# Up products of a hybrid trunk as pairs of 512 and 256 columns with a join, and later ticks for the residual's multiplications

## The chip, the cores and the metric

The kernel runs on one core of a Trainium2 chip. The metric is the device time of one execution in microseconds; before the change the median of three runs is 2261.07 us (2255.51 to 2263.56).

## What is computed

A trunk of two layers over 256 tokens of 2048 features, all in float32. Layer 0 mixes tokens with a bidirectional gated linear attention, layer 1 with a neighbourhood attention over a 4 x 64 grid; each mixer is followed by a gated ConvFFN, and each of the four sub-layers ends in x <- LayerNorm(alpha * x + f(x)). The part the change touches most is the ConvFFN:

```
def _conv_ffn(x, w_up, conv_w, conv_b, w_down):
    h = x @ w_up
    hp = jnp.pad(h, ((0, 0), (1, 1), (0, 0)))
    h = hp[:, :-2] * conv_w[0] + hp[:, 1:-1] * conv_w[1] + hp[:, 2:] * conv_w[2] + conv_b
    a, b = jnp.split(h, 2, axis=-1)
    return (jax.nn.gelu(a, approximate=False) * b) @ w_down
```

w_up has 2048 x 11264 entries, w_down 5632 x 2048.

## The kernel before

**Precision.** TensorE multiplies float32 operands that were rounded to a shorter form (`F32R`). So that little is lost, each operand is split in two: `hi`, its rounded value, made by an ACT copy (L182), and `lo`, what is left, made by a DVE subtraction (L183). A product is then three matmuls: hi by hi, hi by lo and lo by hi, summed in one PSUM bank.

**Weights.** The weights come as units of 128 x 2048 in the order of a plan (`unit_plan`). SP's queue loads them into three raw buffers; `emit_split` splits each into one of four pairs of `hi` and `lo` buffers. The split of a unit is issued when the unit four before it is done (`pump`, `finish`).

**Activations.** `xT` holds the transposed input of a sub-layer as [128, 16 slices of K, 2 token tiles, hi and lo, 128 tokens]; `gT` holds the second operand of the output and down products in the same form.

**Products with the weights held still.** Two helpers multiply a unit of 128 output columns (16 slices of K) by all 256 tokens. `ws_one` (with `ws_part`) serves the q and k units of both mixers: per slice of K one matmul of 512 columns, the `hi` weights by both halves of `xT` (hi and lo side by side), and one of 256, the `lo` weights by the hi half, into the hi half of the bank alone; the two halves of the bank are then added by a join (L578 on ACT, L579 on DVE). `ws_half` serves the up units: per slice three matmuls of 256 columns, all into the same 256 columns, so that nothing has to be joined.

**The ConvFFN.** A layer has 44 channels of 128 for each of the two halves a and b of h. The first two channels come from a block product with transposes (`pair`), the other 84 units from `up_one`, which calls `ws_half`. `evac` takes a unit out of PSUM: `conv` is one ACT pass (L754) and two DVE passes (L755, L756), then a GELU on ACT (L765) for a, and for b the product with the gate on DVE (L769) into `sums`. The down product of the first 32 channels is done in four portions of eight channels by a scheme of seven block products (`seven`, 12 matmuls of 512 columns each, L849) in place of eight; `operands` (L817 to L827) makes their operands from `sums` at the start of a portion. In a portion an up unit stands behind each `seven` unit; the first two up units come ahead of the first `seven`. The results are added to the residual `x_sb` by DVE (`into`, L835). After the portions there are eight more up units and an ordinary down product.

**LayerNorm between sub-layers.** `ln_mid` normalises `x_sb`, transposes it, and splits it into `xT`; the residual itself is multiplied by the norm's gain, four DVE multiplications for each of the two token tiles (`resid`, L392), and the norm's bias is added by a DMA of POOL's queue (L394). These steps are held back by a counter of ticks: `tick` counts pieces of matmul work, and at each tick at most one entry of `slow` that is due is issued.

**The attention.** For each of 16 heads POOL's queue loads a position bias (L896) and adds the mask to it by a second DMA (L897), into one buffer, so that a load waits for the scores of the head before. The scores (L919 and after, on DVE and ACT) need that bias, and TensorE's transposes of the probabilities (L937) need the scores.

**The order of the work.** The program hands its instructions to a scheduler, which sets the order on each engine by priority and by when it reckons that an operand is there; the place in the program is not always the place in an engine's order.

Of the kernel before, what the change touches and what calls it, by code (L numbers as in the profile page):

```python
# [10 lines left out]
F32 = mybir.dt.float32  # L11
# [3 lines left out]
ALU = mybir.AluOpType  # L15
AX = mybir.AxisListType

P = 128
D = 2048
T = 256  # L20
KC = D // P
# [86 lines left out]
def kernel(  # L108
# [16 lines left out]
    nc = tc.nc  # L125
# [15 lines left out]
    def ps_mm():  # L141
        return psum.tile([P, 512], F32, tag="mm", name="ps_mm", bufs=8 - TP)

    def ps_tp():
        return psum.tile([P, 512], F32, tag="tp", name="ps_tp", bufs=TP)

    raws, splits = {}, {}
    st = {"load": 0, "split": 0, "done": 0, "next": 0, "tick": 0}
# [32 lines left out]
    def emit_split(src, hi, lo):  # L181
        nc.scalar.copy(hi, src)  # L182
        nc.vector.tensor_tensor(lo, src, hi.bitcast(F32), ALU.subtract)  # L183
# [32 lines left out]
    def take():  # L216

        pump()
        j = st["next"]
        st["next"] = j + 1  # L220
        return splits.pop(j)

    def finish():
        st["done"] += 1
        pump()

    side, slow = [], []
# [8 lines left out]
    def tick():  # L236
        st["tick"] += 1
        while side and side[0][0] <= st["tick"]:
            side.pop(0)[1]()

        if slow and slow[0][0] <= st["tick"]:
            slow.pop(0)[1]()
# [5 lines left out]
    def mm(o, l, r, start, stop):  # L248
        nc.tensor.matmul(o, l, r, start=start, stop=stop)  # L249


    def ws_part(xs, hi, lo, ps, kcs):
        hi3 = hi.rearrange("p (k m) -> p k m", m=P)
        lo3 = lo.rearrange("p (k m) -> p k m", m=P)
        ps4 = ps.rearrange("p (t h n) -> p t h n", t=2, h=2)
        for kc in kcs:
            mm(ps, hi3[:, kc], xs[:, kc].rearrange("p t h n -> p (t h n)"), kc == 0, False)
            mm(ps4[:, :, 0], lo3[:, kc], xs[:, kc, :, 0], False, kc == KC - 1)

    def ws_half(xs, evac):  # L260

        hi, lo = take()
        ps = ps_mm()[:, :T]
        hi3 = hi.rearrange("p (k m) -> p k m", m=P)
        lo3 = lo.rearrange("p (k m) -> p k m", m=P)
        for kc in range(KC):
            mm(ps, hi3[:, kc], xs[:, kc, :, 0], kc == 0, False)
            mm(ps, hi3[:, kc], xs[:, kc, :, 1], False, False)
            mm(ps, lo3[:, kc], xs[:, kc, :, 0], False, kc == KC - 1)
            if kc % 4 == 3:  # L270
                tick()
        evac(ps)
        finish()

    def ws_one(xs, evac):
        hi, lo = take()
        ps = ps_mm()
        for c in range(4):
            ws_part(xs, hi, lo, ps, range(4 * c, 4 * c + 4))
            tick()  # L280
        evac(ps)
        finish()
# [58 lines left out]
    xT = act.tile([P, KC, 2, 2, P], F32R, tag="xT", name="xT")  # L341
# [12 lines left out]
    def ln_head(pool, xs, t, stats):  # L354
        mv = pool.tile([P, 2], F32, tag="ln_mv", name="ln_mv", bufs=2)
        nc.vector.bn_aggr(mv, stats)
        rstd = pool.tile([P, 1], F32, tag="ln_rs", name="ln_rs", bufs=2)
        rsqrt(rstd, mv[:, 1:2], 1.0, LN_EPS, pool)
        return mv, rstd

    def ln_mid(pool, xs, t, stats, idx, gb):

        def head():
            mv, rstd = ln_head(pool, xs, t, stats)
            for b in range(4):
                blk = xs[:, t, b * 512:b * 512 + 512]
                nc.vector.tensor_scalar(blk, blk, mv[:, 0:1], rstd, ALU.subtract, ALU.mult)  # L367

        cell = {}

        def turn(b):
            tp = ps_tp()
            for i in range(4):
                kc = 4 * b + i
                nc.tensor.transpose(tp[:, i * P:i * P + P], xs[:, t, kc * P:kc * P + P], ident)  # L375
            if b == 0:
                cell["f"] = pool.tile([P, 4, 4, P], F32, tag="x", name="ln_f")
            f = cell["f"][:, b]
            ks = slice(4 * b, 4 * b + 4)
            with tc.high_priority(offset=LN_BEFORE):  # L380
                for i in range(4):
                    kc = 4 * b + i
                    g_, b_ = lng_sb[:, idx, 0, kc:kc + 1], lng_sb[:, idx, 1, kc:kc + 1]
                    if i % 2 == 0:
                        nc.scalar.activation(f[:, i], tp[:, i * P:i * P + P], AF.Identity, bias=b_, scale=g_)
                    else:
                        nc.vector.tensor_scalar(f[:, i], tp[:, i * P:i * P + P], g_, b_, ALU.mult, ALU.add)  # L387
                emit_split(f, xT[:, ks, t, 0], xT[:, ks, t, 1])

        def resid(b):  # L390
            sl = slice(b * 512, b * 512 + 512)
            nc.vector.tensor_tensor(xs[:, t, sl], xs[:, t, sl], gb[:, sl], ALU.mult)  # L392
            if b == 3:
                nc.gpsimd.dma_start(xs[:, t], lnp[idx, 1:2, :].broadcast_to([P, D]), accum_op=ALU.add)  # L394

        later(head, 0)
        for b, n in enumerate((4, 0, 0, 0)):
            later(lambda b=b: turn(b), n)
        for b in range(4):
            slow.append((st["tick"] + 24 + 5 * b, lambda b=b: resid(b)))  # L400

    gb_ps = {}

# [124 lines left out]
    hi = hi_p.tile([P, 2048], F32R, tag="hi", name="hi")  # L528
    lo = lo_p.tile([P, 2048], F32R, tag="lo", name="lo")
# [211 lines left out]
    def ffn(layer):  # L741
        pool = scope["pool"]
        idx = 2 * layer + 1
# [5 lines left out]
        sums = pool.tile([P, PN, 2, P], F32, name="sums")  # L749

        def conv(i, ch, hh):
            c = pool.tile([P, T], F32, tag=f"c{i}", name="c", bufs=2)
            w_ = cw[:, ch]
            nc.scalar.activation(c, hh, AF.Identity, bias=cb[:, ch:ch + 1], scale=w_[:, 1:2])  # L754
            nc.vector.scalar_tensor_tensor(c[:, 1:], hh[:, :T - 1], w_[:, 0:1], c[:, 1:], ALU.mult, ALU.add)  # L755
            nc.vector.scalar_tensor_tensor(c[:, :T - 1], hh[:, 1:], w_[:, 2:3], c[:, :T - 1], ALU.mult, ALU.add)  # L756
            return c

        gate = {}

        def evac(i, ch, ps):

            c = conv(i, i * NCT + ch, ps)
            if i == 0:
                nc.scalar.activation(c, c, AF.Gelu)  # L765
                gate["a"] = c
            else:
                gg = sums[:, ch % PN]
                nc.vector.tensor_tensor(gg.rearrange("p t n -> p (t n)"), gate["a"], c, ALU.mult)  # L769
                if ch >= PN * (PORTIONS + 1):  # L770
                    k = ch - PN * PORTIONS
                    emit_split(gg, gT[:, k, :, 0], gT[:, k, :, 1])

        def up_one(i, ch):
            ws_half(xT, lambda ps: evac(i, ch, ps))


        ht = {}
# [100 lines left out]
        for ch in range(PN * (PORTIONS + 1), NCT):  # L879
            for i in range(2):  # L880
                up_one(i, ch)
# [187 lines left out]
```

## Time and profile before

| | |
|---|---|
| runs | 2255.51, 2261.07, 2263.56 us |
| profiled execution | 2262.09 us, span 2260.4 us |
| mean granted TensorE clock | 0.998 |
| TensorE busy | 2240.8 us (99%), 14236 matmuls |
| DVE busy | 1600.3 us (71%) |
| ACT busy | 1195.6 us (53%) |
| POOL busy | 151.8 us (7%) |
| DMA | 489.69 MB, 217 GB/s in the mean |

All times in the profile are counted from the start of the span. In a row of the timeline the first number is the start, the second the busy time of what the row holds (x2 is two instructions in a row), and brackets at the end say how long the engine was idle before and what ended it. Matmuls overlap in the pipeline, so that the spacing of their starts says what one costs, and the mean duration does not.

### The profile page before, as it was taken

The page shows a single profiled execution, that of the slowest core. Times are in us where ns is not written, and L with a number is a line of the kernel's source. Part 1 is how long each engine was busy: PE and PEld are TensorE (multiplying, and loading weights), DVE is VectorE, ACT ScalarE, POOL GpSimd, SP SyncE. Part 2 cuts the span into 40 slices and gives each one's busy share as a digit, 9 for nine tenths or more (in the row PEclk, how much of TensorE's full clock was granted, in tenths as well). Part 3 has the DMA queues.
Part 4 walks back from the last instruction along what each step waited for, and adds up shares of the span by engine and source line. Part 5 has one row for each costly group of instructions (what it writes and reads, how often), then busy time and mean ns, then how long its engine had stood idle before and what let it go on. Part 6 is the DMA issues. An engine that isn't in the chain of part 4 may idle for free. (4 is left out here: it accounts for less than half of the span.)

```text
span 2260.4 us, 34682 instructions
## 1 busy us (share of the span) xinstructions
PE 2240.8 (99%) x14236; PEld 2034.1 (90%) x14236; DVE 1600.3 (71%) x2144; ACT 1195.6 (53%) x1625; POOL 151.8 (7%) x200
## 2 busy tenths in 40 slices
PE   9999999999999999999999999999999999999998
PEld 7888888999999999999888888889999999999996
DVE  7656655877777777775676666667877778787765
ACT  6655543555555555554454554445655555555542
POOL 1101000000000000000010100000000000000001
PEclk9999999999999999999999999999999999999999
DMA  8544464858888787865475555547688787878742
GB/s 282 184 174 168 178 236 167 279 180 258 254 237 246 228 256 220 252 218 187 168 259 174 194 189 200 182 167 261 203 251 249 243 246 226 251 225 258 233 187 94
DMA packets 73535, 489.69 MB, mean 217 GB/s; under 512 B 8416, under 2 KB 10720, under 8 KB 15904
## 3 DMA queue, kind: packets, MB, share of 16 engines
q1 hardware_dynamic: 53424, 364.67, 43.6%
q0 software_dynamic: 19664, 122.28, 23.6%
q8 instruction: 112, 1.84, 0.3%
q10 hardware_dynamic: 288, 0.52, 0.1%
q14 instruction: 47, 0.39, 0.0%
HBM read 482.20 MB, written 2.10 MB: 214 GB/s over the span
## 5 line engine op out<-in xcount | busy, mean ns | idle before, releaser
L249 PE MATMUL ps_mm<-xT,hi 128*128 128x256 f32 (+1 forms) x6160 | 1252.8, 298 | 1.2 <-ACT hi L182 0.6
L183 DVE TENSOR_TENSOR lo<-raw,hi 128x1024 fp32r<-128x1024 f32 (+1 forms) x695 | 828.9, 1208 | 498.6 <-ACT hi L182 497.5
L182 ACT CAST hi<-raw 128x1024 fp32r<-128x1024 f32 (+1 forms) x695 | 708.3, 1038 | 757.9 <-PE ps_mm L249 550.6
L249 PEld LDWEIGHTS ps_mm<-xT,hi 128*128 128x128 f32 x6160 | 993.3, 191 | 45.4 <-ACT hi L182 1.8
L249 PE MATMUL ps_mm<-xT,lo 128*128 128x256 f32 x3472 | 981.0, 283 | 0.5 <-DVE lo L183 0.5
L249 PEld LDWEIGHTS ps_mm<-xT,lo 128*128 128x128 f32 x3472 | 663.9, 191 | 1.5 <-DVE lo L183 1.1
L849 PE MATMUL ps_mm<-hi,gT 128*128 128x512 f32 x896 | 295.6, 391 | 0.0
L249 PE MATMUL ps_mm<-hi,xT 128*128 128x512 f32 x896 | 283.8, 391 | 0.3 <-DVE xT L183 0.3
L249 PE MATMUL ps_mm<-hi,gT 128*128 128x512 f32 x896 | 278.3, 390 | 0.0
L249 PEld LDWEIGHTS ps_mm<-hi,xT 128*128 128x128 f32 x896 | 168.1, 188 | 35.6 <-DVE xT L183 1.1
L249 PEld LDWEIGHTS ps_mm<-hi,gT 128*128 128x128 f32 x896 | 168.2, 188 | 34.7
L849 PEld LDWEIGHTS ps_mm<-hi,gT 128*128 128x128 f32 x896 | 168.7, 188 | 33.0
L849 PE MATMUL ps_mm<-lo,gT 128*128 128x512 f32 x448 | 175.7, 392 | 0.0
L249 PE MATMUL ps_mm<-lo,xT 128*128 128x512 f32 x448 | 174.8, 390 | 0.0
L249 PE MATMUL ps_mm<-lo,gT 128*128 128x512 f32 x448 | 174.6, 390 | 0.0
L183 DVE TENSOR_TENSOR lo<-x,hi 128x1024 fp32r<-128x1024 f32 x128 | 151.5, 1218 | 5.6 <-ACT hi L182 5.1
L182 ACT CAST hi<-x 128x1024 fp32r<-128x1024 f32 x128 | 128.6, 1045 | 37.6 <-PE ps_mm L849 12.4
L249 PEld LDWEIGHTS ps_mm<-lo,gT 128*128 128x128 f32 x448 | 84.1, 188 | 17.0
L249 PEld LDWEIGHTS ps_mm<-lo,xT 128*128 128x128 f32 x448 | 84.2, 188 | 16.6
L849 PEld LDWEIGHTS ps_mm<-lo,gT 128*128 128x128 f32 x448 | 84.6, 189 | 13.3
L754 ACT ACTIVATE c<-ps_mm,cb,cw 128x256 f32<-128x256 f32 x168 | 94.1, 560 | 0.0
L835 DVE SCALAR_TENSOR_TENSOR x_sb<-x_sb,ps_mm 128x512 f32<-128x512 f32 x128 | 85.9, 676 | 0.0
(157 smaller groups left out, 1298.5 us busy)
## 6 DMA issues: line engine op xcount, KB each, us to landing
raw<-in_w_dram SPq DMA_DIRECT2D x340, 1024.0 KB, 4.9
x<-in_w_dram POOLq DMA_DIRECT2D x64, 1024.0 KB, 8.1
z<-in_w_dram POOLq DMA_DIRECT2D x32, 1024.0 KB, 8.1
x_sb<-in_lnp_dram POOLq DMA_DIRECT2D x6, 1024.0 KB, 11.1
g<-in_lnp_dram POOLq DMA_DIRECT2D x4, 1024.0 KB, 19.1
raw<-in_w_dram SPq DMA_DIRECT2D x12, 256.0 KB, 6.6
bt<-in_bias_dram POOLq DMA_DIRECT2D x16, 192.0 KB, 2.8
bt<-bmask_sb POOLq DMA_DIRECT2D x16, 192.0 KB, 3.3
```

Of the source, the lines that this page charges most:

```text
L182: nc.scalar.copy(hi, src)
L183: nc.vector.tensor_tensor(lo, src, hi.bitcast(F32), ALU.subtract)
L249: nc.tensor.matmul(o, l, r, start=start, stop=stop)
L754: nc.scalar.activation(c, hh, AF.Identity, bias=cb[:, ch:ch + 1], scale=w_[:, 1:2])
L835: nc.vector.scalar_tensor_tensor(blk, blk, ALPHA if first else 1.0, ps, ALU.mult, ALU.subtract if sub else ALU.add)
L849: nc.tensor.matmul(ps, o[:, kc, l], r[:, kc], start=new and kc == 0 and n == 0, stop=kc == 3 and n == 2, skip_group_check=not new)
```

## The change

Up units go through `ws_one` in place of `ws_half`, which falls away: 16 matmuls of 512 columns and 16 of 256 in place of 48 of 256. `evac` gets an argument `parts`: an ACT copy takes the second half of the bank to a new SBUF tile `h`, a DVE addition adds the first half to it in place, and the convolution reads `h` instead of the bank. The channels of `pair` still go to the convolution straight from their bank. The tile of the second gate half (`c1`) has one buffer in place of two. In `ln_mid`, for the norm between the first ConvFFN and the attention (`idx == 1`), the ticks at which the residual's multiplications come due are 36 + 8b in place of 24 + 5b.

```diff
@@ -256,21 +256,6 @@
         for kc in kcs:
             mm(ps, hi3[:, kc], xs[:, kc].rearrange("p t h n -> p (t h n)"), kc == 0, False)
             mm(ps4[:, :, 0], lo3[:, kc], xs[:, kc, :, 0], False, kc == KC - 1)
-
-    def ws_half(xs, evac):
-
-        hi, lo = take()
-        ps = ps_mm()[:, :T]
-        hi3 = hi.rearrange("p (k m) -> p k m", m=P)
-        lo3 = lo.rearrange("p (k m) -> p k m", m=P)
-        for kc in range(KC):
-            mm(ps, hi3[:, kc], xs[:, kc, :, 0], kc == 0, False)
-            mm(ps, hi3[:, kc], xs[:, kc, :, 1], False, False)
-            mm(ps, lo3[:, kc], xs[:, kc, :, 0], False, kc == KC - 1)
-            if kc % 4 == 3:
-                tick()
-        evac(ps)
-        finish()
...
@@ -397,7 +382,7 @@
         for b in range(4):
-            slow.append((st["tick"] + 24 + 5 * b, lambda b=b: resid(b)))
+            slow.append((st["tick"] + (36 + 8 * b if idx == 1 else 24 + 5 * b), lambda b=b: resid(b)))
...
@@ -749,7 +734,7 @@
         def conv(i, ch, hh):
-            c = pool.tile([P, T], F32, tag=f"c{i}", name="c", bufs=2)
+            c = pool.tile([P, T], F32, tag=f"c{i}", name="c", bufs=2 - i)
...
@@ -758,8 +743,15 @@
-        def evac(i, ch, ps):
-
+        def evac(i, ch, ps, parts=False):
+
+            if parts:
+                h = pool.tile([P, T], F32, tag="h", name="h", bufs=2)
+                h3 = h.rearrange("p (t n) -> p t n", t=2)
+                ps4 = ps.rearrange("p (t h n) -> p t h n", t=2, h=2)
+                nc.scalar.copy(h3, ps4[:, :, 1])
+                nc.vector.tensor_tensor(h3, ps4[:, :, 0], h3, ALU.add)
+                ps = h
             c = conv(i, i * NCT + ch, ps)
...
@@ -772,7 +764,7 @@
         def up_one(i, ch):
-            ws_half(xT, lambda ps: evac(i, ch, ps))
+            ws_one(xT, lambda ps: evac(i, ch, ps, True))
```

The order that the scheduler builds shows the change at three places. The lines of the changed kernel are lower by 15 from `ws_one` on, and by 8 after `evac`.

TensorE at the seam between a `seven` unit (L849, after the change L841) and the next up unit (L249), in the first portion; before:

```order
L849 MATMUL ps_mm<-lo,gT 128x512
L849 MATMUL ps_mm<-hi,gT 128x512
L249 MATMUL ps_mm<-xT,hi 128x256 x2
L249 MATMUL ps_mm<-xT,lo 128x256
L249 MATMUL ps_mm<-xT,hi 128x256 x2
L249 MATMUL ps_mm<-xT,lo 128x256
```

and after the change, in the same place:

```order
L841 MATMUL ps_mm<-lo,gT 128x512
L841 MATMUL ps_mm<-hi,gT 128x512
L249 MATMUL ps_mm<-xT,hi 128x512
L249 MATMUL ps_mm<-xT,lo 128x2x128
L249 MATMUL ps_mm<-xT,hi 128x512
L249 MATMUL ps_mm<-xT,lo 128x2x128
```

Each pair of 256-column products with the `hi` weights has become one of 512; nothing else on TensorE has moved between the units.

DVE at the start of the first ConvFFN's last portion, where `operands` (L819 to L827, after the change L811 to L819) follows the last up unit of the portion before; before:

```order
L183 TENSOR_TENSOR lo<-raw,hi 128x1024
L755 SCALAR_TENSOR_TENSOR c<-ps_mm,cw,c 128x255
L183 TENSOR_TENSOR lo<-raw,hi 128x1024
L756 SCALAR_TENSOR_TENSOR c<-ps_mm,cw,c 128x255
L769 TENSOR_TENSOR sums<-c 128x256
L819 TENSOR_TENSOR sums<-sums 128x4x128
L823 TENSOR_TENSOR sums<-sums 128x4x128
```

and after the change:

```order
L183 TENSOR_TENSOR lo<-raw,hi 128x1024
L753 TENSOR_TENSOR h<-ps_mm,h 128x256
L183 TENSOR_TENSOR lo<-raw,hi 128x1024
L740 SCALAR_TENSOR_TENSOR c<-h,cw,c 128x255
L741 SCALAR_TENSOR_TENSOR c<-h,cw,c 128x255
L761 TENSOR_TENSOR sums<-c 128x256
L811 TENSOR_TENSOR sums<-sums 128x4x128
L815 TENSOR_TENSOR sums<-sums 128x4x128
```

The addition of the join stands where the first pass of the convolution stood, between the two halves of a split, and both passes come behind the second half. On ACT the copy of the join stands between the two roundings of that split, and the convolution's pass behind the second.

DVE at the start of the attention, with the last of the residual's multiplications (L392, after the change L377) ahead of the first head's scores (L919, after the change L911); before:

```order
L392 TENSOR_TENSOR x_sb<-x_sb,g 128x512 x2
L183 TENSOR_TENSOR lo<-raw,hi 128x1024
L579 TENSOR_TENSOR qk<-ps_mm,join_t 128x256
L183 TENSOR_TENSOR lo<-raw,hi 128x1024
L183 TENSOR_TENSOR q<-qk,q 128x256
```

and after the change:

```order
L377 TENSOR_TENSOR x_sb<-x_sb,g 128x512 x2
L183 TENSOR_TENSOR lo<-raw,hi 128x1024
L564 TENSOR_TENSOR qk<-ps_mm,join_t 128x256
L183 TENSOR_TENSOR lo<-raw,hi 128x1024
L183 TENSOR_TENSOR q<-qk,q 128x256
```

From the end of the first ConvFFN to the end of the attention the rows of all five engines read alike, but for line numbers.

## Rows read from the trace of the kernel before

**Rows 1.** The page: busy time, share and count; the chain that ended last.
```profile
PE 2240.8 (99%) x14236; PEld 2034.1 (90%) x14236; DVE 1600.3 (71%) x2144; ACT 1195.6 (53%) x1625; POOL 151.8 (7%) x200
...
PE ps_mm L249 38%; PE ps_mm L849 7%; PE ps_tp L249 1%; DMA bt<-bmask_sb 0%; PE ps_tp L937 0%; PE ps_tp L375 0%; DVE lo L183 0%; DVE x_sb L367 0%; DVE ln_st L463 0%; DVE x_sb L417 0%; POOLq L1065 0%; DVE ln_f L387 0%; POOL x_sb L424 0%; PE ps_tp L790 0%; ACT x_sb L422 0%
```

**Rows 2.** Waits (total, times, longest): TensorE's longest in all; DMA's in 424 to 1066.
```profile
PE ps_tp L937 <- DVE s L930: 4.0, 1, 4.0
...
ACT hi L182 <- DMA raw<-in_w_dram: 9.2, 3, 4.7
...
ACT hi L182 <- DMA x<-in_w_dram: 2.7, 2, 2.0
```

**Rows 3.** Busy time by stretch: a portion, and four microseconds of the attention.
```profile
core 0: us, PE busy (x) PEld busy (x) DVE busy (x) ACT busy (x) POOL busy (x), PEclk, DMA share, GB/s
625.70:756.20 130.50, 130.50 (x939) 123.63 (x938) 101.29 (x128) 73.42 (x92) 9.16 (x12) 1.00 0.82 242
1190.70:1194.70 4.00, 4.00 (x17) 3.41 (x18) 2.47 (x5) 2.25 (x5) 0.86 (x1) 0.62 0.66 145
```

**Rows 4.** Timeline of TensorE: a `seven` unit, an up unit, the next `seven`.
```profile
902.39 0.62 PE L849 MATMUL ps_mm<-hi,gT 128*128 128x512 f32 x2
...
904.44 0.39 PE L849 MATMUL ps_mm<-hi,gT 128*128 128x512 f32 x1
904.67 0.40 PE L249 MATMUL ps_mm<-xT,hi 128*128 128x256 f32 x2
...
910.42 0.40 PE L849 MATMUL ps_mm<-hi,gT 128*128 128x512 f32 x1
```

**Rows 5.** Timeline of TensorE: 44 pairs of `ws_one` in the attention, behind 512-column matmuls.
```profile
1380.20 0.39 PE L249 MATMUL ps_mm<-xT,hi 128*128 128x512 f32 x1
...
1380.89 0.40 PE L249 MATMUL ps_mm<-xT,hi 128*128 128x512 f32 x1
...
1381.25 0.40 PE L249 MATMUL ps_mm<-xT,hi 128*128 128x512 f32 x1
...
1385.84 0.40 PE L249 MATMUL ps_mm<-xT,hi 128*128 128x512 f32 x1
...
1395.73 0.44 PE L249 MATMUL ps_tp<-k,q 128*128 128x256 f32 x2
```

**Rows 6.** Timeline of TensorE: eight pairs of `ws_one` behind 256-column products.
```profile
1270.46 0.39 PE L249 MATMUL ps_mm<-xT,hi 128*128 128x512 f32 x1
...
1273.23 0.87 PE L249 MATMUL ps_tp<-k,q 128*128 128x256 f32 x6
```

**Rows 7.** Groups of instructions: busy us, mean ns of one, idle before.
```profile
L754 ACT ACTIVATE c<-ps_mm,cb,cw 128x256 f32<-128x256 f32 x168 | 94.1, 560 | 0.0
...
L765 ACT ACTIVATE c<-c 128x256 f32<-128x256 f32 x88 | 36.4, 413 | 36.0 <-DVE c L756 36.0
...
L578 ACT COPY join_t<-ps_mm 128x256 f32<-128x256 f32 x48 | 17.4, 362 | 2.9 <-issue 2.1 <-PE ps_mm L249 0.8
...
L579 DVE TENSOR_TENSOR qk<-ps_mm,join_t 128x256 f32<-128x256 f32 x32 | 13.4, 420 | 0.1
```

**Rows 8.** Timeline of DVE inside a portion, after an up unit.
```profile
911.58 1.23 DVE L183 TENSOR_TENSOR lo<-raw,hi 128x1024 fp32r<-128x1024 f32 x1 [2.49 <-ACT hi L182]
912.73 0.47 DVE L755 SCALAR_TENSOR_TENSOR c<-ps_mm,cw,c 128x255 f32<-128x255 f32 x1
```

**Rows 9.** Timeline at a portion's start: DVE's last operand, TensorE's first `seven`.
```profile
890.92 0.68 DVE L183 TENSOR_TENSOR gT<-sums,gT 128x512 fp32r<-128x512 f32 x1
...
893.42 0.40 PE L849 MATMUL ps_mm<-hi,gT 128*128 128x512 f32 x1
```

**Rows 10.** Timeline of DVE and TensorE in the attention: the second head's scores.
```profile
1186.89 0.76 DVE L919 SCALAR_TENSOR_TENSOR s<-ps_tp,bt 128x256 f32<-128x256 f32 x2 [7.17 <-DMA bt<-bmask_sb]
...
1191.51 0.52 PE L249 MATMUL ps_mm<-xT,hi 128*128 128x512 f32 x1
...
1194.59 0.60 PE L249 MATMUL ps_mm<-xT,hi 128*128 128x512 f32 x1
```

## The prediction

> **What bounds the kernel now.** Read the page's busy shares first: TensorE is busy for 2240.8 of 2260.4 us, DVE for 71% of the span, and the chain that ended last consists of TensorE's matmuls at L249 and L849 [rows 1]. A busy TensorE is not yet a TensorE that works at the shortest spacing, so the second view is what it waits for: in the whole program one wait of 4.0 us, in the attention, and in the first ConvFFN's 642 us ACT waited 9.2 + 2.7 us in all for weights that a DMA brought, TensorE not at all [rows 2]. The third is a table by stretch: one ConvFFN portion is 130.50 us long, TensorE fills it, and DVE has 101.29 us of work in it, ACT 73.42, the DMA engines a share of 0.82 [rows 3]. So in the ConvFFN the time is the number of matmuls times their spacing, and the spacing is read from starts in the timeline, not from the mean durations of the groups (those overlap).
>
> There a `seven` unit's nine 512-column matmuls from 902.39 to 904.44 take 2.05 us, 0.228 each; the up unit behind it starts at 904.67 and the next `seven` unit at 910.42: 5.75 us for 48 matmuls of 256 columns, 0.120 each [rows 4]. Half the columns cost more than half the time: 2 x 0.120 = 0.240 against 0.228.
>
> **The change, part by part.**
>
> *The matmuls.* An up unit issues, for each of 16 slices of K, two products of 256 columns with the same weights and one with others. Now the two are one of 512 columns: 48 matmuls become 32, the columns stay. The attention's q and k units already run that form, through `ws_one`, so its price is in the trace. Where such a run follows 512-column matmuls, as nearly all up units do (behind `seven`, or behind another up unit), the first pair starts at 1380.20 and the seventeenth at 1385.84: 5.64 us for the 16 pairs of a unit; 44 pairs to 1395.73 take 15.53 us, 0.353 each, so it does not drift [rows 5]. Behind the attention's short products of 256 columns, eight pairs from 1270.46 to 1273.23 take 2.77 us, 0.346 each [rows 6]. That makes 5.54 us a unit. I take 5.64, because what stands ahead of the up units is what stands ahead of the run in [rows 5]; 5.54 is the low bound. The high bound is the slowest pair in the timeline of that run: 1380.89 to 1381.25, 0.36, that is the 3 x 0.120 of now and no gain.
>
> The gain is 5.75 - 5.64 = 0.11 us for each of the 168 units (the count of L754 on `ps_mm` [rows 7]): **18.5 us**. By the two bounds: 168 x 0.21 = 35 us, and nothing.
>
> The Trainium skill speaks against this size. Its page "TensorE: Matmul & The Clock Gate", section "Back-to-back issue gap", gives N / 2.4 + 2.5 ns for a warm matmul: 109 ns for 256 columns and 216 for 512, so that the merger would save 2.5 ns a pair, 168 x 16 x 2.5 ns = 6.7 us (an estimate from that page). The trace shows 120 and 228 instead; the sum goes by the trace.
>
> *The join.* Each unit gets an ACT copy of 128x256 out of PSUM and a DVE addition. The same two stand in the attention at 362 and 420 ns [rows 7]. Per portion (16 units) that is 5.8 us of ACT and 6.7 of DVE: DVE goes to 108.0 of about 128.7 us, 84%, ACT to 79.2, 62% [rows 3, 7]. Within one pair of units DVE sits idle for 2.49 us until ACT's next rounding, whose own release is TensorE giving back a weight buffer [rows 8]; 0.42 more and 0.11 less length leave about 1.9. The splits of a unit start when the unit four before it is done, so they are ready units ahead. I cost the join at nothing; the cover is that idle time, and if it were gone each unit would pay up to 0.78 us, 168 x 0.78 = 131 us. It isn't gone unless DVE loses four times what the join adds.
>
> *The convolution* now reads SBUF where it read PSUM. L754 took 560 ns on PSUM; another ACT pass over 128x256 on SBUF, L765, took 413 [rows 7]. DVE's two passes on SBUF stand nowhere in the trace; between 0.42 (the addition) and their 0.47 now [rows 8]. All of it lies beside TensorE: nothing. The PSUM bank comes free after the addition instead of after the second pass, earlier. The second gate tile lost its spare buffer: its writer waits for the product of the channel before, which is a whole pair of units old.
>
> *The portion boundary* is where the longer way out of PSUM could reach TensorE. `operands()` needs the last channel's product, and the first `seven` unit needs the operands. The last of these ends at 890.92 + 0.68 = 891.60; TensorE takes up that unit at 893.42 [rows 9]. The slack is 1.8 us. The two up units in between shrink by 0.22, the join adds 0.36 + 0.42 = 0.78 (the order now has copy, rounding, convolution on ACT, and addition, split, the two passes on DVE, so part of it hides behind the split). 0.8 us remain: no wait.
>
> *The residual's multiplications.* The ticks of the eight DVE multiplications at the attention's start go from 24 + 5b to 36 + 8b. But the order built for DVE shows them at the very places they had before, ahead of the first head's scores, and from there to the attention's end no row of any engine or queue moved, POOL's and SP's DMAs included. The scheduler had pulled them forward and still does. I cost it at zero, and with it stays what goes wrong there: the bias of the second head lands late, DVE waits 7.17 us for it, TensorE 4.00 [rows 10], and then runs for some microseconds at a mean granted clock of 0.62 [rows 3], partly at the lower level, 1.2 GHz.
>
> **The sum** against the profiled execution, 2262.09 us (span 2260.4 and 1.7 around it): 2262.1 - 18.5 + 0 = 2243.6. That run lies 1.0 above the median of 2261.07, so the median should come to **about 2243 us**, -0.8%.
>
> **The rivals.**
>
> *The fast spacing everywhere.* If the up units settle at 0.346, as in [rows 6], the gain is 35 us: 2226. For it: the runs of the first FFN units follow short transposes. Against: nothing in [rows 5] leaves 0.353 in 44 pairs, and 140 of the 168 units come after the first `seven` of their layer, behind 512 columns or behind other up units.
>
> *Columns alone count.* If each pair took the 0.36 of the slowest pairs, or a matmul cost its columns and next to nothing beside, as the page named above has it, the time would be 2254 to 2261: no change. Against it stand 0.228 and 0.120 [rows 4], and that two of three pairs in [rows 5] are at 0.35.
>
> *Slower: the wait at the portion boundary.* If on ACT the copy falls behind one more rounding (1.05) and on DVE the addition behind one more split (1.22), the chain grows by 0.78 + 2.27 = 3.05, the slack of 1.6 is spent and TensorE waits 1.45 us at each of 8 boundaries. That alone is 12 us and would only halve the gain. It decides from 2.3 us a boundary (18.5 / 8), a chain longer by 3.9. With a wait like the attention's 4.0, and the slow pairs behind it (five take 3.08 us from 1191.51 to 1194.59 [rows 10], 1.3 more than at 0.353), a boundary costs 5.3 and all eight 42: about 2286. Against it: the order puts the addition directly behind the first split.
>
> *The change of ticks does act*, though no row moved: without the wait of 4.0 and the slow pairs the time would be 5.3 us lower still, 2238.
>
> **How the numbers follow.** Forecast 0.80; fast spacing everywhere 0.08; ticks that act 0.02; columns alone 0.05; part of the gain lost in boundary waits, so that less than 0.3% is left, 0.02; slower 0.03. A measurement of this kernel can tell about 0.3% (6.8 us) from no change. So faster 0.90, same 0.07, slower 0.03. The range: upward 4 us for half a microsecond at each boundary, and 4 for the spread of the runs (2255.51 to 2263.56): 2251. Downward 8 us if half of the units run at 0.346 (84 x 0.10), and 4 of spread: 2231.
>
> **What would show it.** TensorE should have 2688 matmuls fewer, and an up unit from its first matmul to the next `seven` should last 5.64 us (5.54 in the fast case, 5.75 if only columns count). A portion should last 128.7 us instead of 130.5. The matmuls at L849's place should start with no wait in the releasers, and DVE should still show idle time ahead of the first split of each pair. The wait of the second head should be there again, about 4 us. The prediction is wrong if a portion is longer than 130 us, if TensorE shows waits on DVE's operand splits, or if the sum of pairs is right and the attention or the seams between stages changed by several microseconds.

## Result and the profile after

The changed kernel takes **2246.93 us** in the median of five runs (2245.65 to 2247.35). The kernel before, run beside it, takes 2261.07 (2255.51 to 2263.56). The ratio is 0.9941, interval 0.9924 to 0.9958: faster by 14.1 us, 0.6%. The profiled execution took 2247.35 us (span 2245.6), 14.7 less than that of before.

Busy time in the changed kernel, from its profile page:

```profile
PE 2222.8 (99%) x11548; PEld 1889.9 (84%) x11548; DVE 1660.4 (74%) x2312; ACT 1258.2 (56%) x1793; POOL 150.8 (7%) x200
```

Against [rows 1], TensorE has 2688 matmuls fewer, which is 168 units of 16. DVE has 60 us more work and ACT 63, and TensorE is still the engine that is never free.

The timeline of TensorE, to be read beside [rows 4]: the last matmuls of a `seven` unit, the up unit, the next `seven` unit (L841 is L849 of before):

```profile
500.20 0.40 PE L841 MATMUL ps_mm<-hi,gT 128*128 128x512 f32 x1
...
502.93 0.39 PE L249 MATMUL ps_mm<-xT,hi 128*128 128x512 f32 x1
...
503.27 0.40 PE L249 MATMUL ps_mm<-xT,hi 128*128 128x512 f32 x1
...
503.62 0.40 PE L249 MATMUL ps_mm<-xT,hi 128*128 128x512 f32 x1
...
503.99 0.40 PE L249 MATMUL ps_mm<-xT,hi 128*128 128x512 f32 x1
...
508.57 0.40 PE L841 MATMUL ps_mm<-hi,gT 128*128 128x512 f32 x1
```

From 502.93 to 508.57 an up unit lasts 5.64 us (5.75 before). After the first of 0.34 the pairs in it take 0.35, 0.35 and 0.36 us by turns (starts are rounded to 0.01), 0.3525 in the mean; the run of [rows 5] has the same rhythm.

The groups of ACT and DVE that form and read the join, to be read beside [rows 7]:

```profile
L739 ACT ACTIVATE c<-h,cb,cw 128x256 f32<-128x256 f32 x168 | 101.1, 602 | 59.8 <-DVE h L753 59.6
...
L752 ACT COPY h<-ps_mm 128x256 f32<-128x256 f32 x168 | 61.4, 365 | 0.0
...
L741 DVE SCALAR_TENSOR_TENSOR c<-h,cw,c 128x255 f32<-128x255 f32 x168 | 80.4, 479 | 1.5
...
L753 DVE TENSOR_TENSOR h<-ps_mm,h 128x256 f32<-128x256 f32 x168 | 70.0, 417 | 0.0
```

Where the time went shows in a table by stretch, from the last transposes of a ConvFFN's first channels to its last down product (the first row is the first ConvFFN, the second row the second), and for the first four heads of the attention, from the first head's scores to the fourth's last product (third row). The first number after the window is its length. Before the change:

```profile
423.67:1126.13 702.46, 701.97 (x4989) 662.80 (x4988) 521.04 (x669) 380.79 (x485) 37.55 (x50) 1.00 0.75 232
1549.58:2249.49 699.91, 699.91 (x4973) 661.23 (x4972) 515.15 (x661) 376.13 (x478) 40.36 (x53) 1.00 0.74 228
1166.75:1221.94 55.19, 51.19 (x288) 44.32 (x286) 33.83 (x59) 28.19 (x52) 5.71 (x8) 0.97 0.68 224
```

and after it:

```profile
423.45:1116.57 693.12, 692.62 (x3654) 591.16 (x3652) 551.33 (x753) 412.24 (x569) 37.57 (x50) 1.00 0.76 234
1541.69:2234.76 693.07, 691.40 (x3637) 589.54 (x3636) 545.16 (x745) 407.57 (x562) 40.41 (x53) 1.00 0.75 230
1157.12:1214.05 56.93, 51.60 (x287) 44.60 (x286) 34.15 (x59) 28.21 (x52) 5.71 (x8) 0.94 0.66 217
```

The first ConvFFN gained 9.34 us, the second only 6.84, and the four heads lost 1.74: together 14.4 of the 14.8 us by which the span shrank. So two things are to be explained: the 2.5 us that the second ConvFFN lacks, and the attention. TensorE's waits name both places (total, times, longest; beside [rows 2]):

```profile
PE ps_tp L929 <- DVE s L922: 5.3, 1, 5.3
...
PE ps_mm L841 <- ACT gT L182: 1.2, 1, 1.2
```

**In the attention** the second head's bias lands late once more. This is [rows 10] in the changed kernel, with the end of the wait on TensorE:

```profile
1178.82 0.75 DVE L911 SCALAR_TENSOR_TENSOR s<-ps_tp,bt 128x256 f32<-128x256 f32 x2 [8.43 <-DMA bt<-bmask_sb]
...
1182.54 1.09 PE L929 MATMUL ps_tp<-ident,s 128*128 128x128 f32 x4 [5.26 <-DVE s L922]
```

DVE waits 8.43 us for it (7.17 before) and TensorE 5.26 (4.00 before). Behind it the pairs are slow again, at a mean granted clock of 0.70 (the number ahead of the last two):

```profile
1184.00:1188.00 4.00, 4.00 (x20) 3.50 (x19) 1.81 (x3) 2.29 (x4) 0.00 (x0) 0.70 1.00 307
```

**In the second ConvFFN** the wait on L841 is that at the start of its first portion:

```profile
1618.81 0.28 PE L249 MATMUL ps_mm<-xT,lo 128*128 128x256 f32 x1
1620.29 0.50 PE L841 MATMUL ps_mm<-hi,gT 128*128 128x512 f32 x1 [1.20 <-ACT gT L182]
...
1621.28 0.74 PE L841 MATMUL ps_mm<-hi,gT 128*128 128x512 f32 x2 [0.26 <-DVE gT L183]
```

The first portion of that ConvFFN lasts 129.38 us from its first `seven` unit to the next portion's; the five others that can be measured so last 128.71 each (130.52 before, in all six).

### The profile page after: what moved, and what is told of

It is laid out like the page before. It is cut to its first block, busy times and chain, and to the rows that moved or that the text cites. A ratio compares the mean times of both kernels' runs of the same rounds, so it can differ in the third digit from the quotient of the medians.

```text
span 2245.6 us, 29529 instructions
## 1 busy us (share of the span) xinstructions
PE 2222.8 (99%) x11548; PEld 1889.9 (84%) x11548; DVE 1660.4 (74%) x2312; ACT 1258.2 (56%) x1793; POOL 150.8 (7%) x200
## 5 line engine op out<-in xcount | busy, mean ns | idle before, releaser
L249 PE MATMUL ps_mm<-xT,hi 128*128 128x512 f32 x3472 | 1235.2, 399 | 1.8 <-ACT hi L182 1.4
L249 PE MATMUL ps_mm<-xT,lo 128*128 128x256 f32 x3472 | 974.9, 281 | 0.4 <-DVE lo L183 0.4
L249 PEld LDWEIGHTS ps_mm<-xT,hi 128*128 128x128 f32 x3472 | 652.5, 188 | 161.4 <-ACT hi L182 2.5
L249 PEld LDWEIGHTS ps_mm<-xT,lo 128*128 128x128 f32 x3472 | 656.0, 189 | 6.0 <-DVE lo L183 1.1
L841 PE MATMUL ps_mm<-hi,gT 128*128 128x512 f32 x896 | 295.7, 391 | 1.5 <-ACT gT L182 1.2
L249 PE MATMUL ps_mm<-hi,xT 128*128 128x512 f32 x896 | 283.8, 391 | 0.2 <-DVE xT L183 0.2
L249 PE MATMUL ps_mm<-hi,gT 128*128 128x512 f32 x896 | 278.4, 390 | 0.0
L841 PEld LDWEIGHTS ps_mm<-hi,gT 128*128 128x128 f32 x896 | 168.2, 188 | 40.3 <-ACT gT L182 1.5
L249 PEld LDWEIGHTS ps_mm<-hi,xT 128*128 128x128 f32 x896 | 168.1, 188 | 35.6 <-DVE xT L183 1.1
L249 PEld LDWEIGHTS ps_mm<-hi,gT 128*128 128x128 f32 x896 | 168.2, 188 | 34.7
L841 PE MATMUL ps_mm<-lo,gT 128*128 128x512 f32 x448 | 175.6, 392 | 0.0
L249 PE MATMUL ps_mm<-lo,xT 128*128 128x512 f32 x448 | 174.8, 390 | 0.0
L249 PE MATMUL ps_mm<-lo,gT 128*128 128x512 f32 x448 | 174.6, 390 | 0.0
L182 ACT CAST hi<-x 128x1024 fp32r<-128x1024 f32 x128 | 127.9, 1039 | 17.8 <-DMA x<-in_w_dram 15.4
L739 ACT ACTIVATE c<-h,cb,cw 128x256 f32<-128x256 f32 x168 | 101.1, 602 | 59.8 <-DVE h L753 59.6
L249 PEld LDWEIGHTS ps_mm<-lo,gT 128*128 128x128 f32 x448 | 84.1, 188 | 17.0
L249 PEld LDWEIGHTS ps_mm<-lo,xT 128*128 128x128 f32 x448 | 84.2, 188 | 16.5
L841 PEld LDWEIGHTS ps_mm<-lo,gT 128*128 128x128 f32 x448 | 84.1, 188 | 13.3
L827 DVE SCALAR_TENSOR_TENSOR x_sb<-x_sb,ps_mm 128x512 f32<-128x512 f32 x128 | 86.9, 679 | 0.0
```

Of the source, the lines that this page charges most:

```text
L827: nc.vector.scalar_tensor_tensor(blk, blk, ALPHA if first else 1.0, ps, ALU.mult, ALU.subtract if sub else ALU.add)
L841: nc.tensor.matmul(ps, o[:, kc, l], r[:, kc], start=new and kc == 0 and n == 0, stop=kc == 3 and n == 2, skip_group_check=not new)
```

## The experiments

The theory at the start: the gain is the spacing of TensorE's matmuls and nothing else, the join is free, and the rest of the difference to the forecast sits in waits that the change did not make. Rivals: the join costs part of the gain, or the ticks do. Each ratio below is against the kernel before as it ran beside that experiment, with a median of 2263.13 us for experiments 1 to 4, 2256.53 for 5 and 2256.4 for 6 to 9; so compare the experiments by their times, not by their ratios.

**1. The join alone, with the old matmuls.** The unit again issues three matmuls of 256 columns per slice, but into two halves of the bank, so that the join is needed.

```diff
+    def ws_three(xs, evac):
...
+        for kc in range(KC):
+            mm(ps4[:, :, 0], hi3[:, kc], xs[:, kc, :, 0], kc == 0, False)
+            nc.tensor.matmul(ps4[:, :, 1], hi3[:, kc], xs[:, kc, :, 1], start=False, stop=False, skip_group_check=True)
+            mm(ps4[:, :, 0], lo3[:, kc], xs[:, kc, :, 0], False, kc == KC - 1)
...
-            ws_one(xT, lambda ps: evac(i, ch, ps, True))
+            ws_three(xT, lambda ps: evac(i, ch, ps, True))
```

> The three matmuls of 256 columns are kept and the join is added: hi by hi and lo by hi go to one half of the bank, hi by lo to the other, and the new evac adds the halves. Theory (the whole gain is TensorE's spacing, the join lies beside it): an up unit lasts 5.75 us as before, a ConvFFN portion 130.5 us, the time is 2262 us, plus up to 3 us for waits in the second ConvFFN. Rival (the new spacing is worth more than 18.5 us and the join eats a part of it): portions of 131 us or more, 2267 us or more.

Measured: 2262.0 us in ten runs, ratio 0.9998 (0.9986 to 1.0009). An up unit lasts 5.75 us (504.55 to 510.30), as before. The two ConvFFNs:

```profile
423.60:1126.06 702.46, 701.97 (x4989) 662.82 (x4988) 551.53 (x753) 412.04 (x569) 37.48 (x50) 1.00 0.75 231
1547.80:2248.39 700.59, 700.33 (x4974) 661.19 (x4972) 545.21 (x745) 407.14 (x562) 40.30 (x53) 1.00 0.74 228
```

The first is as long as before the change to 0.01 us, so there the join and the convolution on SBUF cost nothing. The second is 0.68 us longer, nearly all of it in its first portion, too little to show in the time. The whole gain is TensorE's new form of the products.

**2. Like shapes side by side.** The forecast's two bounds for a pair were 0.353 and 0.346 us. If the alternation of 512 and 256 columns makes the difference, every second slice with its 256-column product ahead should give the lower one.

```diff
-            mm(ps, hi3[:, kc], ..., kc == 0, False)
-            mm(ps4[:, :, 0], lo3[:, kc], xs[:, kc, :, 0], False, kc == KC - 1)
+            both = lambda: mm(ps, hi3[:, kc], ..., kc == 0, kc == KC - 1)
+            one = lambda: mm(ps4[:, :, 0], lo3[:, kc], xs[:, kc, :, 0], False, False)
+            for f in (both, one) if kc % 2 == 0 else (one, both):
+                f()
```

> As the changed kernel, but in every second slice of K the matmul of 256 columns comes ahead of the one of 512, in all units of ws_one, so that columns run 512, 256, 256, 512, 512 and so on. Theory (a pair of 512 and 256 costs 0.353 us only because the two kinds alternate; next to their own kind they cost 0.227 and 0.120): 0.347 a pair, an up unit 5.55 us instead of 5.64, 168 x 0.09 = 15 us less in the ConvFFNs and some 3 in the q and k units, 2229 us. Rival (the pair's price is set by its columns and weight loads in any order): 5.64 us a unit, 2247 us.

Measured: 2229.9 us (2229.25 to 2230.32), ratio 0.9861 (0.9838 to 0.9885). The timeline of TensorE, one up unit:

```profile
501.83 0.39 PE L249 MATMUL ps_mm<-xT,hi 128*128 128x512 f32 x1
502.06 0.40 PE L249 MATMUL ps_mm<-xT,lo 128*128 128x256 f32 x2
502.29 0.63 PE L249 MATMUL ps_mm<-xT,hi 128*128 128x512 f32 x2
502.76 0.39 PE L249 MATMUL ps_mm<-xT,lo 128*128 128x256 f32 x2
502.99 0.62 PE L249 MATMUL ps_mm<-xT,hi 128*128 128x512 f32 x2
...
507.40 0.39 PE L843 MATMUL ps_mm<-hi,gT 128*128 128x512 f32 x1
```

From 501.83 to 507.40 a unit takes 5.57 us, 0.348 a pair, with the same matmuls, columns and weights. In the up units the order of the matmuls alone makes this difference. The two ConvFFNs:

```profile
423.42:1109.16 685.74, 685.22 (x3652) 588.07 (x3651) 554.89 (x753) 405.64 (x569) 37.53 (x50) 1.00 0.76 237
1532.58:2217.61 685.03, 683.77 (x3636) 586.40 (x3635) 548.78 (x745) 401.17 (x562) 40.38 (x53) 1.00 0.75 233
```

They are 7.38 and 8.04 us shorter than in the changed kernel, 15.4 of the 17 us (0.09 a unit in the mean of the first one). The edit reaches the q and k units of both mixers too.

The alternation of shapes is not the whole cause, though. The first layer of the kernel before has 36 pairs of `ws_one` in a row, alternating 512 and 256 columns; here are its first matmul and the one behind its last:

```profile
99.00 0.40 PE L249 MATMUL ps_mm<-xT,hi 128*128 128x512 f32 x1
...
111.49 0.39 PE L249 MATMUL ps_mm<-hi,xT 128*128 128x512 f32 x1
```

That is 12.49 us, 0.347 a pair. With the pairs turned the same 36 pairs take 12.55, 0.349:

```profile
98.72 0.40 PE L249 MATMUL ps_mm<-xT,hi 128*128 128x512 f32 x1
...
111.27 0.39 PE L249 MATMUL ps_mm<-hi,xT 128*128 128x512 f32 x1
```

So the alternating order ran in two rhythms, 0.347 and 0.353 us a pair, and the up units behind a `seven` unit were all in the slower one; the turned order took 0.348 to 0.349 in both places. What puts a run into one rhythm or the other, and what in the engine makes them, no run here isolates.

**3. The gain load held back.** In the norm ahead of the attention POOL's queue issues a load of 1 MB for the gain of the norm behind the attention, long before it is used. Here the scheduler may not pull it forward.

```diff
-        nc.gpsimd.dma_start(g, lnp[idx, 0:1, :].broadcast_to([P, D]))
+        d = nc.gpsimd.dma_start(g, lnp[idx, 0:1, :].broadcast_to([P, D]))
+        if idx == 2:
+            tc.keep_in_program_order(d)
```

> As the changed kernel, but the load of the norm's gain for the attention's output (1 MB, POOL's queue) keeps its place in the program, behind the attention, where the scheduler had pulled it to the start. The residual's DMAs stay where they are. Theory (two loads of 1 MB ahead of the second head's bias make it late, the gain's load being one): the wait of 5.3 us in the attention shrinks by more than half, 2242 us. Rival (the residual's DMA alone makes it late): the wait stays above 4 us, 2246 us.

Measured: 2241.01 us, one run. The row that waited for 8.43 us:

```profile
1172.88 0.76 DVE L913 SCALAR_TENSOR_TENSOR s<-ps_tp,bt 128x256 f32<-128x256 f32 x2 [2.76 <-DMA bt<-bmask_sb]
```

TensorE no longer waits for the scores. This is more than expected: in this run holding the gain load alone was enough.

**4. The residual's two DMAs held back as well.** Same edit, and `keep_in_program_order` for the two DMAs of 1 MB that add the norm's bias to `x_sb` (`idx == 1`).

> As the changed kernel, but both the gain's load and the two DMAs that add the norm's bias to the residual keep their places in the program on POOL's queue, behind the first four heads' biases: what the later ticks say and the scheduler undid. Theory: no wait for the second head's bias, the 5.3 us and the slow pairs behind it (1.3 to 1.7 us) go, 2240 us. Rival (the bias is late by its own two steps, each behind SP's weight loads): the wait stays, 2247 us.

Measured: 2240.6 us (2239.52 to 2241.42), ratio 0.9909 (0.9889 to 0.9929): no better than the gain load alone. The DMA issues from 1120 to 1185, size and median us to landing, of the changed kernel:

```profile
x_sb<-in_lnp_dram POOLq DMA_DIRECT2D x2, 1024.0 KB, 10.1
g<-in_lnp_dram POOLq DMA_DIRECT2D x1, 1024.0 KB, 16.9
bt<-in_bias_dram POOLq DMA_DIRECT2D x3, 192.0 KB, 9.0
bt<-bmask_sb POOLq DMA_DIRECT2D x3, 192.0 KB, 8.2
```

and of this one, with the length of its first four heads:

```profile
bt<-in_bias_dram POOLq DMA_DIRECT2D x3, 192.0 KB, 2.7
bt<-bmask_sb POOLq DMA_DIRECT2D x3, 192.0 KB, 3.1
...
1156.80:1206.21 49.41, 49.41 (x287) 43.13 (x286) 33.82 (x58) 28.15 (x52) 6.65 (x9) 1.00 0.70 209
```

A bias of 192 KB lands in about a third of the time when the loads of 1 MB are out of its way, and the four heads take 49.41 us in place of 56.93. The weight loads on SP's queue land sooner too (5.0 us in the median, 8.5 in the changed kernel), so the delay is not confined to POOL's queue; whether the order in that queue or the shared DMA engines make it was not separated.

**5. The same two holds on the kernel before.** This asks whether the spread of the kernel before is that wait, and what the up products are worth without it.

> The kernel before, with the gain load and the two residual additions of the norm ahead of the attention kept in program order; nothing else. Theory (the two groups of times that the kernel before shows, near 2256 and near 2263 us, differ by the second head's bias wait, which is there in one and mostly absent in the other; the stretch of the first four heads took 55.2 us in the profiled run of before against 49.1 to 49.2 of the like stretches behind it, 6.0 us too long): no wait of TensorE in the attention, first four heads 49.4 us, all runs within 2 us of each other, median 2255.5 to 2256.5, so that the up products alone are worth the distance to the same two holds on the changed kernel, 2240.6, about 15.5 us. Rival (the two groups come from elsewhere): the wait goes, but the runs still lie in two groups some 7 us apart, and the median is lower than 2256 by several microseconds in the fast group. The sum of the prediction, 18.5 us, would put it at 2259; with the 2.5 to 4 us that the second ConvFFN of the changed kernel loses it agrees with the theory.

Measured: 2256.34 us in ten runs, all within 2255.84 to 2257.46; ratio 0.9987 (0.9975 to 1.0). The kernel before, in thirteen runs beside it, came out eight times between 2255.6 and 2257.17 and five times between 2261.85 and 2264.78. With the loads held the upper group is gone and the lower one is left. The first four heads take 49.50 us in place of 55.19, with no wait of TensorE for the scores, and both ConvFFNs are as long as before (702.46 and 699.91):

```profile
1166.60:1216.10 49.50, 49.50 (x289) 43.23 (x287) 33.92 (x58) 28.25 (x52) 7.66 (x10) 1.00 0.80 240
```

So the upper group is the late bias. That it costs nearly nothing in the lower group follows from the times; no trace of a run of that group was taken. Between the two kernels with the loads held the up products are worth 2256.34 - 2240.6 = 15.7 us. What is missing of the 18.5 lies again in the second ConvFFN, which in the profiled execution of experiment 4 was only 5.23 us shorter than before the change:

```profile
1533.87:2228.55 694.68, 692.03 (x3638) 590.59 (x3636) 545.38 (x745) 407.50 (x562) 40.50 (x53) 1.00 0.74 229
```

**6. The old ticks.** `36 + 8 * b if idx == 1 else 24 + 5 * b` goes back to `24 + 5 * b`; the order of the instructions on all engines is that of the changed kernel.

> As the changed kernel, with the residual's ticks as they were before (24 + 5b in all layers). The order of every engine and queue, waits included, is the same with both. Theory (the change of ticks does nothing): 2246 to 2247.5 us, the wait of the second head between 4.5 and 5.5 us. Rival (it acts in a way that the order does not show): a difference of more than 2 us, or a wait outside that range.

Measured: 2249.09 us, one run. The wait of the second head is 5.3 us, as with the new ticks. The time is 2 us above the median of the changed kernel. Of this 1.1 us lies in the second ConvFFN, where TensorE's wait at the first portion is 2.1 us (1.2 and 0.3 in the changed kernel), with the same instructions in the same order. The ticks do nothing that shows; that wait varies between runs with the same instructions. The time misses the theory's 2246 to 2247.5, and the difference is just over the 2 us that the rival named; so the theory rests on the equal order and the equal wait in the attention, not on the time of this one run.

**7. The last norm's gain copied later.** The second ConvFFN has something that the first has not: ACT copies the gain of the last norm into PSUM, and the scheduler puts these copies ahead of its first portion, where the gain has not landed. In the changed kernel (ACT's timeline):

```profile
1565.35 0.59 ACT L396 COPY ps_tp<-g 128x512 f32<-128x512 f32 x1 [7.61 <-DMA g<-in_lnp_dram]
```

and before:

```profile
1572.60 1.63 ACT L411 COPY ps_tp<-g 128x512 f32<-128x512 f32 x3 [4.88 <-DMA g<-in_lnp_dram]
```

Roundings and joins stand behind them on ACT. The experiment keeps the three copies in program order, in the middle of the second portion. The load of the gain moves up in the program with them, but POOL issues it at the same time (1543.37 us, 1543.38 in the changed kernel). From the edit:

```diff
+    def last_g():
+        gb_ps[0] = [ps_tp() for _ in range(3)]
+        for b in range(3):
+            tc.keep_in_program_order(nc.scalar.copy(gb_ps[0][b], scope["gb"][:, b * 512:b * 512 + 512]))
...
+                if p == 1 and n == 8 and idx == 2 * DEPTH - 1:
+                    last_g()
```

> As the changed kernel, but the last norm's copies of its gain to PSUM (three on ACT), which the scheduler had pulled to the start of the second ConvFFN, are held until the middle of its second portion. Theory (ACT's 7.6 us wait for that gain's load puts the splits and convolutions behind, and with the join they have not caught up by the first portion's start): the wait of 7.6 us on ACT, TensorE's waits there (0.5 us at 1568, 1.4 us and half speed for about 2 at 1619) go, 2244 us; the second ConvFFN then gains as much as the first, 9.4 us. Rival (the second ConvFFN's first portion is late because of the weights' loads at its start): the waits stay, 2247 us.

Measured: 2245.29 us (2242.12 to 2246.78), ratio 0.9935 (0.9909 to 0.9961): the gain over the changed kernel is 1.6 us in the median and within the spread of the runs. The trace says it more sharply (the second ConvFFN's stretch):

```profile
1541.68:2232.24 690.56, 690.56 (x3637) 589.66 (x3636) 545.55 (x745) 407.86 (x562) 40.44 (x53) 1.00 0.75 231
```

690.56 us in place of 693.07. That is 9.35 less than before the change, just what the first ConvFFN gained, and the waits of ACT and at the first portion are gone.

**8. The join three times as long.** Two more ACT copies and two more DVE passes over `h` per unit. This tells whether DVE's and ACT's load or the way to the portion boundary is what the join could spoil.

```diff
-                nc.scalar.copy(h3, ps4[:, :, 1])
+                for _ in range(3):
+                    nc.scalar.copy(h3, ps4[:, :, 1])
                 nc.vector.tensor_tensor(h3, ps4[:, :, 0], h3, ALU.add)
+                for _ in range(2):
+                    nc.vector.tensor_tensor(h3, h3, h3, ALU.max)
```

> As the changed kernel, but each join has three ACT copies (of the same half) and two further DVE passes over h (its maximum with itself), so that a unit costs 0.73 us of ACT and about 0.84 us of DVE more. Theory (the join's cost is its length in the chain to the portion boundary, where 1.14 us are left, and not DVE's load): pairs of units inside a portion stay at 8.39 us, each of the 8 boundaries waits 0.5 to 2 us and then runs for a while at half speed, 2253 to 2270 us. Rival A (the cover is ample everywhere): 2247 us. Rival B (DVE's load binds, about 121 of 128.7 us in a portion): the pairs themselves get longer than 8.45 us.

Measured: 2267.2 us, one run. TensorE's waits:

```profile
PE ps_mm L844 <- ACT gT L182: 17.0, 8, 4.6
```

All eight boundaries wait, 2.1 us each in the mean. Inside a portion a `seven` unit and its up unit still start 8.38 us apart (513.37 to 521.75), as in the changed kernel. This is the prediction's rival of the slower kernel, forced: its place was right, and the join as written stays on this side of it.

**9. All of it together.** Turned pairs, both holds and the late copies.

> The changed kernel with the turned pairs, the held loads in the attention and the late copies together. Theory (the three have different causes and add up: 17 from the pairs, 6.3 from the held loads, 2.5 to 3 from the copies): 2246.9 - 26 = 2221 us. Rival (what one gives, another takes back: the portion boundaries, with 1.04 us left, begin to wait): 2225 us or more.

Measured: **2220.85 us** (2220.77 to 2221.05), ratio 0.9828 (0.9809 to 0.9848), faster than both kernels. The stretches, both ConvFFNs and the first four heads:

```profile
423.44:1109.19 685.75, 685.25 (x3652) 588.12 (x3651) 554.78 (x753) 405.71 (x569) 37.73 (x50) 1.00 0.76 237
1524.87:2208.06 683.19, 683.19 (x3636) 586.48 (x3635) 548.97 (x745) 401.36 (x562) 40.54 (x53) 1.00 0.75 233
1149.59:1198.55 48.96, 48.96 (x287) 42.89 (x285) 34.31 (x59) 27.60 (x52) 6.65 (x9) 1.00 0.72 210
```

Both ConvFFNs are 16.7 us shorter than before the change. What the first gains the second gains too, once ACT isn't held up at its start.

## Why the prediction was right, and where it was off

*The matmuls: right in kind and size.* A unit lasts 5.64 us, as taken from [rows 5]. The first ConvFFN, where nothing else interferes, gained 9.34 us; 84 units at 0.11 make 9.24. With the late copies the second gained 9.35. The full 18.5 us are there; 14.1 arrived. Experiment 1 shows that nothing but the new form of the products pays. The rival of the fast spacing was wrong for the up units. The prediction chose 0.353 over 0.346 by what stands ahead of a unit, and behind 512-column matmuls the slower rhythm came every time; but that this is the cause is not shown. Behind the attention's short products there are runs of both kinds (the eight pairs from 1270.46 in [rows 6] at 0.346, the sixteen from 1273.94 at 0.353), and the 36 pairs of experiment 2's comparison, behind the same matmuls, took 12.49 us before and 12.72 in the changed kernel (98.63 to 111.35). So the choice was right by a regularity and not by a known mechanism.

The two ConvFFNs show 18.7 us where no wait interferes (9.34, and 9.35 with the late copies), and the prediction's estimate of 6.7 falls short of that. The Trainium skill's page "TensorE: Matmul & The Clock Gate", section "Back-to-back issue gap", gives N / 2.4 + 2.5 ns as the gap of a single matmul by itself; for a stream with weight loads, such as this one, it says that the formula under-counts at small N and over-counts at large N, so this section does not speak against the size in the way that the prediction took it to. The traces show the formula too low at both widths: 120 ns for 256 columns (109 by the formula) and 228 for 512 (216), and at 512 the measurement decides against the page. The formula also has no term for the order of the matmuls, and that is worth 0.09 us a unit (experiment 2).

*The join: right but for one place.* Zero in the first ConvFFN and 0.68 us in the second, by experiment 1, with DVE at 107 us of a portion's 128.7 (108.0 forecast) and ACT at 79.3 (79.2).

```profile
627.77:756.48 128.71, 128.71 (x682) 109.92 (x681) 106.83 (x145) 79.27 (x107) 9.15 (x12) 1.00 0.83 245
```

*The convolution on SBUF: wrong in sign, without effect.* ACT's pass L739 takes 602 ns where 560 stood and 413 was the neighbour looked at, which is another function over other operands. The two DVE passes are what they were (477 and 479 ns). They lie beside TensorE, as said.

*The portion boundary: right at seven of eight.* Now the last operand ends 1.1 us ahead of the first `seven` unit that uses it; 0.8 was forecast from the 1.8 of [rows 9]. In experiment 1, with the join and the old spacing, it is 1.35, so the join took 0.47 of the slack and not 0.78, and the shorter units took the other 0.2 that the forecast gave them. In the changed kernel's timeline:

```profile
627.09 0.68 DVE L183 TENSOR_TENSOR gT<-sums,gT 128x512 fp32r<-128x512 f32 x1
...
628.91 0.40 PE L841 MATMUL ps_mm<-hi,gT 128*128 128x512 f32 x1
```

At the eighth, the first of the second ConvFFN, TensorE waits 1.20 us and then 0.26 for DVE's split of an operand, which the prediction named as a sign of being wrong. The step that failed is "0.8 us remain: no wait", read at one boundary of the first ConvFFN and taken for all eight. ACT's wait of 4.88 us for the last norm's gain stood in the trace of before, at the second ConvFFN's start, and wasn't read. Before the change ACT and DVE had caught up by the first portion; with two copies and two additions more for each pair of units (0.73 and 0.83 us by the groups above) and a wait of 7.61 they had not. Experiment 7 takes the copies away and the loss goes with them, 2.5 us here; it is 3.6 in experiment 6 and 4.1 in experiment 4, and only 0.7 in experiment 1, with the same join, the old spacing and a wait of 6.16 us for the gain. How the rest divides between the shorter units and the longer wait is open.

*The ticks: right.* No row moved, and experiment 6 finds the order and the wait in the attention unchanged.

*The attention: right that the wait stays, its size off.* "With it stays what goes wrong there" took 4.0 us from one profiled execution as a fixed number. It is 2.4 to 5.7 us over the runs in which it stood, and the four heads lost 1.74. The deeper miss is the baseline: the kernel before has the wait in some of its executions only, and the changed kernel, by its narrow spread and by the traces of it and of experiments 2, 6, 7 and 8, in all that were seen. So the medians charge the change with a late bias that the other partly lacks. Why the changed kernel was late in all that were seen and the one before only at times is open: the instructions are in the same order, and no run isolates it.

*The sum:* 18.5 - 2.5 (the second ConvFFN's start) - 1.7 (the four heads) = 14.3; measured 14.7 in the profiled executions, which both have the wait, and 14.1 in the medians. That the medians agree is partly luck: against the 2256.4 or the 2263.13 that the kernel before showed beside the experiments, the same 2246.93 would have been a gain of 9.5 or 16.2. 2247 lies within the range, 4 us above the forecast.

## What to carry to other kernels

Where TensorE is never free, the spacing of starts is the price list: read it for each order of shapes, not only for each shape, and at several places, since one order can run in two rhythms; then try another order before counting columns. When a slack has to absorb a longer path, read it at every place where the path recurs, the first one of a stage above all, since the engines may still be catching up there. A large load that nobody needs soon costs when it is issued just ahead of a small one that is needed now; a kernel whose times fall into two groups is worth searching for such a wait before any change to it is priced.

## What was not expected of the hardware

- Alternating 512 and 256 columns ran at 0.353 us a pair in the up units and at 0.347 in a run of 36 pairs in the first layer; with like shapes in twos the same matmuls took 0.348 and 0.349. Over the kernel, with the q and k units, the order alone gives 17 us (2246.93 to 2229.9).
- ACT's scaled pass over 128x256 took 602 ns from SBUF and 560 from PSUM; PSUM was the faster source.
- Bias transfers of 192 KB on POOL's queue landed in 8 to 9 us in the median beside loads of 1 MB on the same queue, and in about 3 without them. One such delay cost the four heads 7.5 us, of which TensorE's wait was 5.3; in the rest it ran at a lower granted clock (0.70 in the mean over four microseconds, that is partly at 1.2 GHz; 1.00 in the four from 1192.50).
